# A diffusion transformer in two layers: the value-and-key projection in the score banks with early weights, adaLN tiles in pumps of three and in buffers of their own

## The chip, the cores and the metric

One NeuronCore of a Trainium2 chip runs the whole program as one launch. The metric is the device time of an execution in microseconds (us). Engines are TensorE (PE; its weight loads are PEld), VectorE (DVE), ScalarE (ACT), GpSimd (POOL) and SyncE (SP), which here only issues DMAs, in the order of its queue. Every engine executes its own instructions in order.

## The reference

Two layers of a diffusion transformer over 256 latent and 256 context tokens of width 1024. In each layer:

```
sa, ca, ga, sf, cf, gf = split(silu(c) @ w_ada + b_ada, 6)      # adaLN, also for c_ctx
h = layernorm(x) * (1 + ca) + sa                                # latent and context tokens
aq,ak,av, nq,nk,nv, cq, ckv, kr = split(h @ w_in)               # 2720 columns
group A (6 heads): two softmax maps, p1 - lam * p2, times av, rmsnorm
group B (6 heads): neighbourhood attention with bias, plus context keys
group C (4 heads): q = rmsnorm(cq) @ w_uq, k, v = rmsnorm(ckv) @ w_ukv, shared rotary key kr
x = layernorm(alpha * x + ga * (concat(A, B, C) @ w_out)) * g1 + b1
u = conv3(modulate(x, sf, cf) @ w_up); y = (silu(gate) * val) @ w_down
x = layernorm(alpha * x + gf * y) * g2 + b2
```

The context tokens take the same path in layer 0 (they read only context). The output is the latent stream.

## The kernel before

**Arithmetic.** Every large product is done in three matmuls (`mm3`): both operands are split into a rounded part (hi) and the remainder (lo), and hi*hi, lo*hi and hi*lo are summed. A weight block is loaded into a `raw` tile (128 x 1024 float32, 512 KB), ScalarE casts it to `whi`, VectorE subtracts to `wlo` (`wsplit`). There are 4 `raw` buffers and 3 each of `whi` and `wlo`. PSUM has 3 banks `acc`, one `ada`, 2 `sc` (scores) and 2 `tp` (transposes).

**adaLN.** w_ada comes in tiles of 128 x 1024. For layer 0 the tiles of round "b" (16) and "c" (8) are multiplied on TensorE (`ada`): a "b" tile is two matmuls on two of the four column groups of the array, and the tile of the other column half (`h`) uses the other two. For layer 1, rounds "b" (16), "c" (8) and "d" (8) run on VectorE in layer 0's w_down stage (`ada_vec`): one scalar_tensor_tensor a tile into an accumulator (the first of eight on ScalarE), and after eight tiles TensorE gathers the accumulator with small matmuls into a `tp` bank. `pump(n)` emits the work of the next n tiles; the projections pump `PF` tiles each, the w_down stage `DP` = 2 tiles a block in its first phase and 1 in its second. All these tiles share the four `raw` buffers with the weights.

**Order.** `ORDERS` lists by hand the parts of the attention of each layer (v: values, ck and cq: the compressed key and query of group C with their norms, mk and mq: its keys and queries, aq to bk: queries and keys of A and B, A, B, C: attention, f: the rest of the adaLN tiles). A list scheduler then sets the order on each engine, hoisting instructions past each other. Some sums ("early", `EF` and value block 0) are done while the tokens are still being modulated. `proj_vk` is the projection onto the last value columns and the rotary key of C: per token tile 24 matmuls with 288 columns, weights in three blocks (864, 864 and 576 columns).

**The w_down stage of layer 0** (`token_major`). The first phase sums the first 512 output columns for four token tiles at once, 11 blocks of w_down with 24 matmuls each. Then `gated` multiplies the sums by the gate and adds them into `xr` (two VectorE instructions a token tile), which frees the banks. The second phase takes the other 512 columns, in a pass over token tiles 2 and 3 (11 blocks of 12 matmuls) and one over 0 and 1, each closed by norm and modulation for layer 1.

## Time and profile before

| | us |
|---|---|
| median of 3 runs | 1173.5 |
| their range | 1173.08 to 1174.99 |
| the profiled execution, its own time | 1174.29 |
| its span in the trace | 1172.5 |
| TensorE busy in the span | 1112.0 |
| VectorE, ScalarE busy | 833.3, 590.3 |
| mean granted clock of TensorE | 0.985 |

Busy times are shares of the span that the engines spend on instructions; they overlap. TensorE is the fullest engine, so what counts is where it stands idle or slow, and what it waits for there. In the trace, names such as `raw<-in_w_ada` are destination and source of an instruction, L129 is a line of the kernel (129 to 131 are the three matmuls of `mm3`, 116 and 117 cast and subtraction of a split, 207 the VectorE step and 228 the TensorE matmul of an adaLN tile, 737 the norm's matmul with ones). TensorE's float32 matmuls are counted as several in the trace (x4 there is x2 in the program).

### The profile page before, as it was taken

How to read it: one execution, taken by the hardware profiler on the slowest of the kernel's cores; microseconds unless marked ns; L12 is line 12 of the kernel's file. 1: busy time of each engine (PE TensorE's matmuls, PEld its weight loads, DVE VectorE, ACT ScalarE, POOL GpSimd, SP SyncE). 2: the span in 40 equal slices, each digit the busy share in tenths (PEclk: the TensorE clock that was granted, in tenths of full speed). 3: DMA queues.
4: the chain of work that ended last, by engine and by line, in shares of the span. 5: the costliest groups of instructions: out<-in, count | busy, mean ns of one | idle time of the engine just before them, and what ended most of it. 6: DMA issues, size and time to landing. Idle time of an engine off the chain costs nothing.

```text
span 1172.5 us, 17767 instructions
## 1 busy us (share of the span) xinstructions
PE 1112.0 (95%) x6704; PEld 899.5 (77%) x6704; DVE 833.3 (71%) x1505; ACT 590.3 (50%) x1063; POOL 83.7 (7%) x104
## 2 busy tenths in 40 slices
PE   5999999999998999999999998989999978999997
PEld 4757766677778988887887776878778758999985
DVE  4533677767588986987975568774776777888755
ACT  4235566655548634444441224564664656666531
POOL 0001000003113000000000002120000411000000
PEclk9999999999999999999999999999999997999999
DMA  9487311112143653644548787523112343556562
GB/s 362 187 284 259 126 37 73 37 37 68 64 165 95 211 166 126 202 150 134 186 156 280 258 267 236 167 74 129 59 37 73 104 153 107 181 181 183 203 210 88
DMA packets 58196, 179.17 MB, mean 153 GB/s; under 512 B 7016, under 2 KB 12408, under 8 KB 58112
## 3 DMA queue, kind: packets, MB, share of 16 engines
q1 hardware_dynamic: 58112, 178.05, 45.8%
q8 instruction: 53, 0.87, 0.3%
q14 instruction: 31, 0.25, 0.1%
HBM read 176.94 MB, written 1.08 MB: 152 GB/s over the span
## 4 chain that ended last, share of the span: by engine, by line
PE 79%; DVE 7%; DMA 6%; ACT 3%; issue 3%; POOL 2%; SPq 1%; DVEq 0%; ACTq 0%; POOLq 0%
PE acc L129 20%; PE acc L130 20%; PE acc L131 20%; PE sc L605 6%; PE tp L385 3%; DMA raw<-in_w_down 3%; PE tp L393 3%; PE sc L810 2%; DVE adasc L207 1%; DVE wlo L117 1%; DMA raw<-in_w_ada 1%; ACT whi L116 1%; PE ada L228 1%; POOL xn L337 1%; DMA rawx<-in_w_ada_e 1%
## 5 line engine op out<-in xcount | busy, mean ns | idle before, releaser
L117 DVE TENSOR_TENSOR wlo<-raw,whi 128x1024 fp32r<-128x1024 f32 (+1 forms) x206 | 249.2, 1214 | 147.0 <-ACT whi L116 141.8
L116 ACT CAST whi<-raw 128x1024 fp32r<-128x1024 f32 (+1 forms) x206 | 212.9, 1038 | 264.6 <-PE acc L130 120.7
L129 PE MATMUL acc<-hhi,whi 128*128 128x256 f32 (+1 forms) x960 | 326.4, 341 | 3.6 <-ACT hhi L353 3.5
L130 PE MATMUL acc<-hlo,whi 128*128 128x256 f32 (+1 forms) x960 | 324.8, 339 | 0.5 <-DVE hlo L354 0.3
L131 PE MATMUL acc<-hhi,wlo 128*128 128x256 f32 (+1 forms) x960 | 323.5, 337 | 0.0
L129 PEld LDWEIGHTS acc<-hhi,whi 128*128 128x128 f32 x960 | 183.6, 192 | 28.6 <-issue 6.1
L130 PEld LDWEIGHTS acc<-hlo,whi 128*128 128x128 f32 x960 | 183.7, 192 | 22.3 <-issue 3.6
L131 PEld LDWEIGHTS acc<-hhi,wlo 128*128 128x128 f32 x960 | 183.6, 191 | 21.7 <-issue 4.1
L377 ACT ACTIVATE p<-sc,nm 128x512 f32<-128x512 f32 (+1 forms) x132 | 81.3, 618 | 25.6 <-DVE nm L374 24.1
L374 DVE TENSOR_REDUCE nm<-sc 128x1 f32<-128x512 f32 (+1 forms) x132 | 77.3, 597 | 19.8 <-PE sc L605 16.2
L386 ACT COPY pT<-tp 128x512 f32<-128x512 f32 (+1 forms) x96 | 49.4, 515 | 55.9 <-PE tp L385 55.3
L605 PE MATMUL sc<-stk,stq 32*128 32x512 f32 (+3 forms) x324 | 75.0, 392 | 1.1 <-ACT p L377 0.9
L605 PEld LDWEIGHTS sc<-stk,stq 32*128 32x128 f32 (+1 forms) x324 | 41.5, 183 | 26.4 <-issue 11.9
L1036 ACT ACTIVATE u<-acc,conv 128x256 f32<-128x256 f32 (+1 forms) x94 | 60.8, 647 | 1.4 <-PE acc L131 1.3
L1039 DVE SCALAR_TENSOR_TENSOR u<-acc,conv,u 128x255 f32<-128x255 f32 (+1 forms) x94 | 54.9, 584 | 4.6 <-ACT u L1036 4.6
L207 DVE SCALAR_TENSOR_TENSOR ac<-raw,scT,ac 128x1024 f32<-128x1024 f32 x42 | 53.3, 1278 | 5.8 <-DMA raw<-in_w_ada 5.8
L1040 DVE SCALAR_TENSOR_TENSOR u<-acc,conv,u 128x255 f32<-128x255 f32 (+1 forms) x94 | 55.3, 588 | 2.3
L385 PE MATMUL tp<-ident,p 128*128 128x128 f32 x320 | 52.7, 279 | 0.1
L130 PE MATMUL acc<-wlo,gBhi 128*128 128x512 f32 x133 | 52.2, 393 | 0.5 <-DVE mv L313 0.5
L385 PEld LDWEIGHTS tp<-ident,p 128*128 128x128 f32 x320 | 36.7, 140 | 20.5 <-issue 8.6
L131 PE MATMUL acc<-whi,gBlo 128*128 128x512 f32 x133 | 51.8, 391 | 0.0
L129 PE MATMUL acc<-whi,gBhi 128*128 128x512 f32 x133 | 51.8, 392 | 0.0
(265 smaller groups left out, 1814.6 us busy)
## 6 DMA issues: line engine op xcount, KB each, us to landing
raw<-in_w_up SPq DMA_DIRECT2D x94, 512.0 KB
raw<-in_w_ada SPq DMA_DIRECT2D x80, 512.0 KB
raw<-in_w_down SPq DMA_DIRECT2D x53, 512.0 KB
raw<-in_w_f SPq DMA_DIRECT2D x27, 512.0 KB
rawx<-in_w_ada_e SPq DMA_DIRECT2D x16, 512.0 KB
raw<-in_w_out SPq DMA_DIRECT2D x16, 512.0 KB
rpb<-in_rpb SPq DMA_DIRECT2D x24, 128.0 KB
gate<-scr SPq DMA_DIRECT2D x12, 256.0 KB
```

The source lines that it names most:

```text
L116: S.copy(hi, raw)
L117: V.tensor_tensor(lo, raw, hi.bitcast(F32), ALU.subtract)
L129: T.matmul(o, lhsT=lh, rhs=rh, start=first, stop=False)
L130: T.matmul(o, lhsT=lh, rhs=rl, start=False, stop=False)
L131: return T.matmul(o, lhsT=ll, rhs=rh, start=False, stop=last).ins
L207: V.scalar_tensor_tensor(ac[c], raw, s, ac[c], ALU.mult, ALU.add)
L374: V.reduce_max(nm, sc[:, 0:nk], axis=AX.X, negate=True)
L377: hT["exp"] = S.activation(p[:, 0:nk], sc[:, 0:nk], AF.Exp, bias=nm, accum_out=sums[:, 0:1]).ins
L385: T.transpose(pt[:, 128 * kc:128 * kc + 128], p[:, 128 * kc:128 * kc + 128], ident)
L605: T.matmul(sc[:, 0:nk], lhsT=q[r, a, qs], rhs=k[r, b, 0:nk], start=t == 0, stop=t == 2, tile_position=(r.start, 0))
L1036: S.activation(t, po[:, c], AF.Identity, scale=cw[:, 1:2], bias=cw[:, 3:4])
L1040: V.scalar_tensor_tensor(t3[:, :, 0:255], p3[:, :, 1:], cw[:, 2:3], t3[:, :, 0:255], ALU.mult, ALU.add)
```

## The change

- `PF` goes from 2 to 3. The early parts (`proj_v` and `fm` with sums from before) no longer pump.
- A new pool `ring` of eight tiles `rawr` takes the adaLN rounds e0, e1 and e3 of the start and then layer 0's "b" and "c" tiles, instead of the shared `raw`; `RX` drops to 4. Before the first attention part the remaining tiles are flushed, the ring is closed, and the attention output `mix` is allocated.
- `vk_weights` loads and rounds w_vk ahead: in layer 0 two of its blocks during the last early step, in layer 1 before the first part; the third block goes into `stk` tiles. `proj_vk` puts its sums into the score banks (in layer 1 alternately with `acc`).
- In the w_down stage the tiles of layer 1's adaLN get four buffers of their own, in the space of the second modulated half (`adalo`), with the accumulators in that of the first (`adahi`, before `adasc`).
- In `ORDERS`, layer 1 gets v1 ahead of mq and mk ahead of aq2; layer 0 loses its `f`.

```diff
--- before.py
+++ after.py
@@ -35,12 +35,13 @@
         ("cosk", "sink", "bones", "ones", "m01", "mneg"), ("st", "stq", "stk"), ("p0",), ("vt",))
 
 
-ORDERS = ("v0 ck cq v1 mk aq0 mq ak1 bq2 C1 ak0 aq1 C0 aq2 A0 bk1 ak2 A1 bk2 bq1 f A2 bk0 bq0 v2 B2 B0 W3 B1 W0 W1",
-          "cq v0 ck mq aq1 v1 aq2 mk ak0 ak1 C0 aq0 C1 ak2 f A1 bq0 bk1 A0 bk0 bk2 bq1 A2 bq2 v2 B0 B1 W3 W1 B2 W0")
+ORDERS = ("v0 ck cq v1 mk aq0 mq ak1 bq2 C1 ak0 aq1 C0 aq2 A0 bk1 ak2 A1 bk2 bq1 A2 bk0 bq0 v2 B2 B0 W3 B1 W0 W1",
+          "cq v0 ck v1 mq aq1 mk aq2 ak0 ak1 C0 aq0 C1 ak2 f A1 bq0 bk1 A0 bk0 bk2 bq1 A2 bq2 v2 B0 B1 W3 W1 B2 W0")
 EARLY = (0, 4)
-PF = 2
+PF = 3
 DP = (2, 1)
-RX = 12
+RX = 4
+RING = 8
 XB = (2, 2, 2, 3)
 HMB = (2, 2, 3, 2)
 PRE = ((0, 1),)
@@ -50,8 +51,12 @@
 
 
 class Slices:
-    def __init__(self, ap):
-        self.ap = ap
+    def __init__(self, ap, ring):
+        self.ap, self.ring = ap, ring
+
+    def raw(self, n):
+        self.ring.append(self.ring.pop(0))
+        return self.ring[-1]
 
     def tile(self, shape, dt, tag=None, name=None, bufs=1):
         o = {"ac0": 0, "ac1": 1024, "bada": 2048}[tag]
@@ -143,6 +148,9 @@
             r = mm3(po[:, 256 * e:256 * e + 256], hT["hi"][:, k, tok], hT["lo"][:, k, tok],
                     hi[:, k % 4, :], lo[:, k % 4, :], first and k == ks[0], last and k == ks[-1])
         return r
+
+    def vk_cols(l, k0, n):
+        return I["w_vk"][l, :, 288 * k0:288 * (k0 + n)]
 
     def kview(w, k):
         return [a.rearrange("p (k c) -> p k c", k=k) for a in w]
@@ -182,9 +190,9 @@
     adaT = {}
     garow = {}
 
-    def ada_w(l, r, k, h):
+    def ada_w(l, r, k, h, raw=wraw):
         c0 = ROUNDS[r][0]
-        raw = wraw(1024)
+        raw = raw(1024) if l or r == "d" else next_slot()
         src = I["w_ada"][l, k * P:(k + 1) * P]
         if r[0] == "a":
             src = src[:, 0:2048].rearrange("p (v s c) -> p s v c", v=2, s=2)[:, c0 // 512]
@@ -200,7 +208,7 @@
         for h in range(nh):
             ac = [ap.tile([P, 1024], F32, tag=f"ac{c}", name="ac", bufs=1) for c in conds]
             for k in range(KD):
-                raw = ada_w(l, r, k, h)
+                raw = ada_w(l, r, k, h, getattr(ap, "raw", wraw))
                 for c in conds:
                     s = scT[:, k, c:c + 1]
                     if k:
@@ -416,8 +424,11 @@
             shift(mv, rs)
             S.activation(xin[t], xin[t], AF.Identity, scale=rs[:, 0:1], bias=rs[:, 1:2])
 
+    def next_slot():
+        return ring.tile([P, 1024], F32, tag="rawr", name="rawr", bufs=RING)
+
     def load_round(s):
-        raws = [lp.tile([P, 1024], F32, tag="rawx", name="rawx", bufs=RX) for _ in range(4)]
+        raws = [lp.tile([P, 1024], F32, tag="rawx", name="rawx", bufs=RX) if s == 2 else next_slot() for _ in range(4)]
         for kp, raw in enumerate(raws):
             load(raw, I["w_ada_e"][s, kp])
         return raws
@@ -468,6 +479,8 @@
                 w[0][:, k % 2, 384:640], w[1][:, k % 2, 384:640], k == 0 and e == 0, k == KD - 1 and e == 1)
 
     new_h()
+    ring_st = ExitStack()
+    ring = pool(ring_st, "ring")
     load_x([2, 3])
     ebias = lp.tile([P, 512], F32, name="ebias")
     load(ebias, I["b_ada_e"])
@@ -493,6 +506,8 @@
         if s < 3:
             wes.append(load_early(s + 1))
             raws, nxt = nxt, load_round(s + 2) if s < 2 else None
+        if s == 3:
+            early["vk"] = {k0: kview(wsplit(vk_cols(0, k0, 3), 864), 3) for k0 in (0, 3)}
         if s == 0:
             for n in range(len(EF)):
                 for k in ks:
@@ -521,7 +536,7 @@
     for l in range(L):
         last = l == L - 1
         hst = ExitStack()
-        h2 = pool(hst, f"h2{l}")
+        mix = []
         lam_init = 0.8 - 0.6 * math.exp(-0.3 * l)
         qc = LAT if last else ALL
         nq = 256 if last else 512
@@ -548,7 +563,6 @@
         V.tensor_scalar_mul(nw[:, 0:1], K["nrm"][:, l, 0:1], 1.0 - lam_init)
         V.tensor_scalar_mul(nw[:, 1:3], K["nrm"][:, l, 1:3], C_SCALE)
 
-        mix = [h2.tile([P, KD, nq], F32R, tag=n, name="mix" + n) for n in ("hi", "lo")]
         core = ExitStack()
         ap = Pools([(pool(core, f"at{l}_{i}", "right"), keys) for i, keys in enumerate(CORE)])
         load_tables(ap)
@@ -563,21 +577,29 @@
             for kb in sorted({k // 4 for k in ks}):
                 w[kb] = w.get(kb) or kview(wsplit(I["w_v"][l, u, kb], 1024), 4)
             for pr in (1, 0):
-                pump(PF)
+                if not pos:
+                    pump(PF)
                 po = pos[pr] if pos else acc()
                 for e in range(2):
                     if pr in prs:
                         v_mm(po, w, ks, pr, e, ks[0] == 0, e == 1 or ks[0] == 0)
                 S.copy(vt[:, 2 * pr:2 * pr + 2, c0:c0 + 256], po.rearrange("p (t c) -> p t c", t=2))
 
+        def vk_weights():
+            vkw.update(early.pop("vk", None) or {k0: kview(wsplit(vk_cols(l, k0, 3), 864), 3) for k0 in (0, 3)})
+            raw = wraw(576)
+            load(raw, vk_cols(l, 6, 2))
+            hi, lo = (st_k().rearrange("p a c -> p (a c)")[:, 0:576] for _ in range(2))
+            split_from(raw, hi, lo)
+            vkw[6] = kview((hi, lo), 2)
+
+        vkw = {}
+
         def proj_vk():
-            w = {}
-            for k0 in (0, 3, 6):
-                n = min(3, KD - k0)
-                w[k0] = kview(wsplit(I["w_vk"][l, :, 288 * k0:288 * (k0 + n)], 288 * n), n)
+            w = vkw
             for t in (2, 3, 0, 1):
                 tok = slice(128 * t, 128 * t + 128)
-                po = acc()
+                po = acc() if last and t % 2 else scp()
                 for k in range(KD):
                     hi, lo = w[k // 3 * 3]
                     mm3(po[:, 0:288], hT["hi"][:, k, tok], hT["lo"][:, k, tok], hi[:, k % 3, :], lo[:, k % 3, :],
@@ -590,7 +612,6 @@
                 po, w, rest = early.pop(i)
                 k0 = 0 if w else 4
                 w = w or kview(wsplit(I["w_f"][l, i, :, 512:1024], 512), 4)
-                pump(PF)
                 for c, ks in rest:
                     f_mm(po, w, k0, ks, c, False, c == CTX)
                 return po
@@ -839,7 +860,14 @@
                  "ak": proj_ak, "bq": proj_bq, "bk": proj_bk, "A": attn_a, "B": attn_b, "C": attn_c, "f": flush}
         seq = ORDERS[l].split()
         for n, part in enumerate(seq):
+            if part[0] in "ABC" and not mix:
+                flush()
+                ring_st.close()
+                h2 = pool(hst, f"h2{l}")
+                mix.extend(h2.tile([P, KD, nq], F32R, tag=v, name="mix" + v) for v in ("hi", "lo"))
             cc["early"] = n < EARLY[l]
+            if not n:
+                vk_weights()
             parts[part.rstrip("0123")](*map(int, part[len(part.rstrip("0123")):]))
         with tc.issue_after(hT["exp"]):
             S.preload_act_table_set("silu_and_others")
@@ -1114,7 +1142,9 @@
         pq = pool(fst, f"pq{l}", "right")
         g2, b2 = lnrow(pq, "ln2_g", l), lnrow(pq, "ln2_b", l)
         if not last:
-            sc = Slices(h1.tile([P, KD, 512], F32R, tag="hi", name="adasc").bitcast(F32).rearrange("p k c -> p (k c)"))
+            free = [h1.tile([P, KD, 512], F32R, tag=n, name="ada" + n).bitcast(F32).rearrange("p k c -> p (k c)")
+                    for n in ("hi", "lo")]
+            sc = Slices(free[0], [free[1][:, 1024 * i:1024 * i + 1024] for i in range(4)])
             pend.extend([ada_vec(l + 1, "b", sc, (0,)), ada_vec(l + 1, "c", sc, (0,)), ada_vec(l + 1, "d", sc, (0,))])
 
         def head2(t):
```

Three places show how this moves instructions. The first is TensorE's order behind the early sums of layer 0 (`sc<-ehi`), before the change: adaLN tiles (`ada`), the norm's matmuls with `ones`, then the first of the w_vk sums (128x288).

```order
L131 MATMUL sc<-ehi,hlo 128x256
L228 MATMUL ada<-raw,scT 32x512 x8
L737 MATMUL tp<-csq,ones 128x512 x2
L228 MATMUL ada<-raw,scT 32x512 x4
L129 MATMUL acc<-whi,hhi 128x288
L737 MATMUL tp<-csq,ones 128x512
L130 MATMUL acc<-wlo,hhi 128x288
L131 MATMUL acc<-whi,hlo 128x288
```

And after it, the w_vk sums follow at once, into `sc`:

```order
L135 MATMUL sc<-elo,hhi 128x256
L136 MATMUL sc<-ehi,hlo 128x256
L134 MATMUL sc<-whi,hhi 128x288
L135 MATMUL sc<-wlo,hhi 128x288
L136 MATMUL sc<-whi,hlo 128x288
L134 MATMUL sc<-whi,hhi 128x288
L135 MATMUL sc<-wlo,hhi 128x288
```

The first adaLN matmuls now come behind 48 such sums (x4, that is two tiles), then x6, x6, and, among the sums of a later part, three tiles cut into pieces:

```order
L136 MATMUL acc<-whi,stk 128x256
L236 MATMUL ada<-rawr,scT 32x512
L134 MATMUL acc<-whi,stk 128x256
L135 MATMUL acc<-wlo,stk 128x256
L136 MATMUL acc<-whi,stk 128x256
L236 MATMUL ada<-rawr,scT 32x512 x4
L134 MATMUL acc<-whi,stk 128x256
L135 MATMUL acc<-wlo,stk 128x256
L136 MATMUL acc<-whi,stk 128x256
```

So tiles that came in pairs now come in threes, and those of one pump are split by the scheduler. In all 12 "b" tiles stand behind the early sums, before and after.

The second place is the w_down stage of layer 0. SyncE's queue before, behind the first three adaLN tiles of the stage, takes blocks and tiles in turn:

```order
L105 DMA raw<-in_w_ada 128x1024
L105 DMA raw<-in_w_down 128x1024
L105 DMA raw<-in_w_ada 128x1024 x2
L105 DMA ln_g<-in_ln_g 128x1024
L105 DMA ln_b<-in_ln_b 128x1024
L105 DMA raw<-in_w_down 128x1024
L105 DMA raw<-in_w_ada 128x1024 x2
L105 DMA raw<-in_w_down 128x1024
L105 DMA raw<-in_w_ada 128x1024 x2
```

After it, the loads from the last of w_up on are:

```order
L110 DMA raw<-in_w_up 128x1024
L110 DMA raw<-in_w_down 128x1024 x6
L110 DMA adalo<-in_w_ada 128x1024 x5
L110 DMA ln_g<-in_ln_g 128x1024
L110 DMA ln_b<-in_ln_b 128x1024
L110 DMA adalo<-in_w_ada 128x1024 x5
L110 DMA raw<-in_w_down 128x1024
L110 DMA adalo<-in_w_ada 128x1024 x2
L110 DMA raw<-in_w_down 128x1024
```

Six blocks go ahead of the first tile, and the first `adalo` waits for the last matmul that reads the second modulated half, at the end of w_up. In VectorE's order the end of the first phase was, with the split of a block (`wlo`), adaLN steps (`adasc`) and the gated sums (`gate`, `xr`):

```order
L117 TENSOR_TENSOR wlo<-raw,whi 128x1024
L207 SCALAR_TENSOR_TENSOR adasc<-raw,scT,adasc 128x1024
L117 TENSOR_TENSOR wlo<-raw,whi 128x1024
L869 TENSOR_TENSOR acc<-acc,gate 128x512
L207 SCALAR_TENSOR_TENSOR adasc<-raw,scT,adasc 128x1024
L870 SCALAR_TENSOR_TENSOR xr_3469,rsum<-xr_3469,acc 128x512
L869 TENSOR_TENSOR acc<-acc,gate 128x512
L869 TENSOR_TENSOR ada<-ada,gate 128x512
```

and is now:

```order
L215 SCALAR_TENSOR_TENSOR adahi<-adalo,scT,adahi 128x1024 x2
L122 TENSOR_TENSOR wlo<-raw,whi 128x1024
L215 SCALAR_TENSOR_TENSOR adahi<-adalo,scT,adahi 128x1024 x3
L122 TENSOR_TENSOR wlo<-raw,whi 128x1024
L215 SCALAR_TENSOR_TENSOR adahi<-adalo,scT,adahi 128x1024
L897 TENSOR_TENSOR acc<-acc,gate 128x512 x2
L898 SCALAR_TENSOR_TENSOR xr_3473,rsum<-xr_3473,acc 128x512
L898 SCALAR_TENSOR_TENSOR xr_3475,rsum<-xr_3475,acc 128x512
L897 TENSOR_TENSOR ada<-ada,gate 128x512
```

An adaLN step stood between the first gated sum and its addition into `xr`; now the last step stands ahead of all the gated sums, and three steps stand ahead of the split before it.

The third place is TensorE's order at the start of layer 1. Before, behind the last early value sums (`sc<-hhi`), came the norm's matmul and the queries of C (`acc<-stq`):

```order
L129 MATMUL sc<-hhi,whi 128x256
L130 MATMUL sc<-hlo,whi 128x256
L131 MATMUL sc<-hhi,wlo 128x256
L737 MATMUL tp<-csq,ones 128x512
L129 MATMUL acc<-stq,whi 128x256 x3
L130 MATMUL acc<-stq,whi 128x256
```

After it the w_vk sums follow, and the norm's matmul stands among them:

```order
L136 MATMUL sc<-whi,hlo 128x288
L134 MATMUL sc<-whi,hhi 128x288
L135 MATMUL sc<-wlo,hhi 128x288
L758 MATMUL tp<-csq,ones 128x512
L136 MATMUL sc<-whi,hlo 128x288
L134 MATMUL sc<-whi,hhi 128x288
L135 MATMUL sc<-wlo,hhi 128x288
```

The queries of C (`acc<-stq`) now come behind all 96 w_vk sums; the first of those stands directly behind the early sums.

## Rows read from the trace of the kernel before

**Rows 1.** The page: busy us of engines, share of span, instructions.

```profile
PE 1112.0 (95%) x6704; PEld 899.5 (77%) x6704; DVE 833.3 (71%) x1505; ACT 590.3 (50%) x1063; POOL 83.7 (7%) x104
```

**Rows 2.** Windows: busy us (instructions) by engine, granted clock, DMA share, GB/s.

```profile
50.00:75.00 25.00, 22.11 (x120) 12.57 (x118) 7.97 (x20) 8.31 (x16) 0.00 (x0) 0.99 0.61 198
400.00:425.00 25.00, 25.00 (x112) 20.72 (x111) 23.59 (x28) 9.86 (x14) 0.00 (x0) 1.00 0.64 198
775.00:800.00 25.00, 20.71 (x142) 19.46 (x141) 14.64 (x27) 12.35 (x26) 5.38 (x6) 0.93 0.31 93
```

**Rows 3.** TensorE timeline after the early sums: start, us, tiles, count, [idle <-releaser].

```profile
65.17 2.46 PE L228 MATMUL ada<-raw,scT 128*32 128x512 f32 x16
67.87 1.96 PE L737 MATMUL tp<-csq,ones 128*128 128x512 f32 x4 [0.24 <-DMA ones<-in_ones]
70.44 1.05 PE L228 MATMUL ada<-raw,scT 128*32 128x512 f32 x4 [0.61 <-DMA raw<-in_w_ada]
71.74 1.05 PE L228 MATMUL ada<-raw,scT 128*32 128x512 f32 x4 [0.25 <-DMA raw<-in_w_ada]
73.90 0.37 PE L129 MATMUL acc<-whi,hhi 128*128 128x288 f32 x1 [1.10 <-ACT whi L116]
74.95 2.07 PE L737 MATMUL tp<-csq,ones 128*128 128x512 f32 x2 [0.69 <-ACT csq L734]
77.06 0.44 PE L131 MATMUL acc<-whi,hlo 128*128 128x288 f32 x1
...
78.21 0.30 PE L130 MATMUL acc<-wlo,hhi 128*128 128x288 f32 x1
...
80.55 1.06 PE L228 MATMUL ada<-raw,scT 128*32 128x512 f32 x8
81.55 0.40 PE L129 MATMUL acc<-whi,hhi 128*128 128x288 f32 x1
```

**Rows 4.** Timeline of TensorE in layer 0's w_down stage, its begin, middle and end.

```profile
607.41 0.50 PE L129 MATMUL acc<-whi,gAhi 128*128 128x512 f32 x1
...
669.79 0.39 PE L129 MATMUL acc<-whi,gChi 128*128 128x512 f32 x1
...
671.60 0.39 PE L131 MATMUL acc<-whi,gClo 128*128 128x512 f32 x1
675.53 0.76 PE L129 MATMUL acc<-whi,gAhi 128*128 128x512 f32 x1 [3.54 <-DVE xr L870]
...
711.74 0.61 PE L131 MATMUL acc<-whi,gClo 128*128 128x512 f32 x2
```

**Rows 5.** Waits of TensorE from 600 to 750 us: total, times, longest.

```profile
PE tp L215 <- DVE adasc L207: 1.5, 2, 1.2
```

**Rows 6.** Timeline of VectorE at the end of the first phase.

```profile
672.12 0.69 DVE L869 TENSOR_TENSOR acc<-acc,gate 128x512 f32<-128x512 f32 x1
673.49 1.28 DVE L207 SCALAR_TENSOR_TENSOR adasc<-raw,scT,adasc 128x1024 f32<-128x1024 f32 x1 [0.67 <-DMA raw<-in_w_ada]
```

**Rows 7.** Windows of 5 us in the same stage, columns as before.

```profile
620.00:625.00 5.00, 5.00 (x23) 4.14 (x23) 0.47 (x2) 0.00 (x0) 0.00 (x0) 1.00 0.99 322
675.00:680.00 5.00, 4.47 (x13) 3.61 (x14) 5.00 (x11) 0.00 (x0) 0.00 (x0) 0.66 0.80 270
```

**Rows 8.** DMA view, 600 to 712 us: what was moved.

```profile
DMA packets 8339, 28.81 MB, mean 257 GB/s; under 512 B 931, under 2 KB 1187, under 8 KB 8335
...
raw<-in_w_ada SPq DMA_DIRECT2D x30, 512.0 KB
```

**Rows 9.** Timeline of SyncE's queue: when adaLN tiles are asked for.

```profile
586.95 5.68 SPq L105 DMA_DIRECT2D raw<-in_w_ada  x2
```

**Rows 10.** Waits of TensorE from 764 to 812 us.

```profile
PE acc L129 <- ACT stq L121: 2.7, 1, 2.7
PE tp L737 <- ACT csq L734: 1.5, 1, 1.5
PE sc L810 <- DVE stk L370: 0.8, 1, 0.8
```


## The prediction

> **What bounds the kernel now.** I began with the busy line of the page: TensorE is at work for 1112.0 of the 1172.5 us of the span [rows 1], so nothing else can be worth more than some 60 us, and a change that leaves TensorE's work alone can only fill holes. The second view was the busy time in windows, to see where the holes are. A window of the middle is full, 25.00 of 25 us, while 50 to 75 holds 22.11 and 775 to 800 only 20.71 [rows 2]; what is gained before a full window is carried through it to the end, because TensorE has no slack there to give back. The third view was TensorE's timeline in the three places that the diff touches: the start of layer 0, the w_down stage of layer 0, the start of layer 1.
>
> Start of layer 0: between 65.17 us, where the early sums end, and 77.06, where the key-and-value sums at last run on, there are five idle spells, of 0.24, 0.61, 0.25, 1.10 and 0.69 us, for the table of ones, for adaLN tiles, for the rounded w_vk and for the squares of the norm [rows 3].
>
> The w_down stage of layer 0: its first matmul is at 607.41, the first of the second half at 675.53 behind a wait of 3.54 us for the gated sum, the last of the pass over tokens 2 and 3 at 711.74 and 0.23 later, twice, so that the pass ends near 712.2 [rows 4]. At full clock eight matmuls lie between 669.79 and 671.60, 0.226 us each. The work is 11 x 24 = 264 matmuls, 59.7 us, and 11 x 12 = 132, 29.9 us: dense, it would end at 697.0. So 15.2 us are lost. What is known of them: 3.7 from 671.8 to 675.5; a wait for the adaLN accumulator, 1.2 at the longest [rows 5]; and a granted clock of 0.66 from 675 to 680 [rows 7], which is the lower level, 1.2 GHz, for two thirds of the window, right after the idle spell.
>
> Start of layer 1: waits of 2.7, 1.5 and 0.8 us [rows 10].
>
> **The start of layer 0.** The change puts the 96 sums of w_vk straight behind the early sums and moves the six adaLN tiles and the norm's ones-matmuls among and behind them. What the 11.9 us from 65.17 to 77.06 hold as work: six tiles, which at the price of a pair (80.55 to 81.55, 1.00 us for two tiles [rows 3]) are 3.0; six ones-matmul passes at 1.96 / 4 = 0.49, 2.9; two first key sums, 0.3. That is 6.2, so 5.7 are there to be won if everything is ready in time. It should be: w_vk no longer stands behind adaLN tiles in SyncE's queue, and the three casts and three subtractions that move ahead fit into 50 to 75, where VectorE works 7.97 and ScalarE 8.31 of 25 us [rows 2]. If they came in the way of the modulated tokens there, up to 2 us would go.
>
> Against it stands the pump of three. Two "b" tiles share one pass, as they use different column groups: two tiles take 1.06 us (80.55), and a lone tile takes 1.05 (70.44, 71.74) [rows 3]. By the order 12 such tiles follow after the early sums; in pumps of two they are 6 passes, in pumps of three (pair and lone, lone and pair) and with the one that the scheduler splits 9. Three passes more at 1.00 are 3.0 us. The copies out of the score banks have a cover: two banks alternate, and a bank has 3.1 us before it is wanted again (the other's 24 sums; 17 of them go from 78.21 to 80.55, 0.13 to 0.14 each [rows 3]); without that it is some 0.5 us at two places, which I leave at nothing. Net gain: 5.7 - 3.0 = **2.7 us**, between 0 and 5.7.
>
> **The w_down stage.** What is removed is the shared buffer: adaLN tiles no longer hold back w_down blocks, nor blocks tiles. What is added is a late start: the tiles lie where the second modulated half was, so that the first can be asked for only after the last w_up matmul, near 607.4; before, the first two were asked for at 586.95 [rows 9]. And VectorE's order changes: the gated sum stands, as before, behind an adaLN step that waits for its tile, now that of tile 23. Behind that step are queued the four gated sums, then the subtractions for blocks 14 and 15; TensorE waits for the first sum into xr, as only that frees its bank.
>
> So when is tile 23 there? Ahead of it in SyncE's queue after 607.4 are 22 tiles, two ln rows and w_down blocks 7 to 15: with itself 34 transfers of 0.524 MB (512 KB, [rows 8]) and a bias of 0.26, together 18.1 MB. They begin to flow near 609 (1.5 us allowed for the queue; each us more or less moves the result by as much). The rate is the open price. Over 600 to 712 the mean is 257 GB/s [rows 8], but that has gaps, as queue and buffers wait for each other; a window with the engines busy 0.99 of the time moved 322 [rows 7]. I take 300, nearer the full window since four buffers keep the queue filled, and keep 270 and 322 for the range. At 300 the tile lands at 609 + 60.3 = 669.3; the step takes 1.28, the gated sum 0.69 [rows 6], and the next one and the sum into xr behind it about as much, 0.6 from start to start: TensorE goes on near 672.6 instead of 675.5. Then 29.9 us of pass, 1.5 for the same drop of the clock (two thirds of 5 us at half speed), and about 2 for blocks whose subtraction stands behind an adaLN step: 706.0 instead of 712.2. Gain: **6.2 us**. At 322 the tile lands at 665.2, ahead of the end of the first half at 667.1; some 0.5 between the halves, no drop: 699.5, gain 12.7. At 270 it lands at 676.0, TensorE goes on at 679.4, and with 4 us of waits the pass ends at 714.8: 2.6 lost. The tail of the stage (norm, modulation, both as before) I leave as it is.
>
> The Trainium skill, "DMA: Bandwidth & Descriptors", section Bandwidth, gives 341 GB/s for one megabyte and 425 for sixteen, and some 358 as the limit of a core at the memory. The trace's full window, 322, is close below the first. By 341 the tile would land at 662 (an estimate), and the whole would come to 1154.1, as at 322.
>
> **The start of layer 1.** The value-and-key sums, 96 of 0.13 us, now stand between the early sums and the first sums that need the normed query; the ones-matmul comes after 11 of them. So the waits of 2.7 and 1.5 us get 12.5 us of cover, and the 0.8 of the first score goes, since w_vk no longer follows the keys: 5.0. Something is late next: a score row of the C heads now stands right behind the key sums and waits for their rotation and copies; I take 1.0 for it, from the 0.8 that such a wait costs now [rows 10]. If w_vk's cast is late (it needs the buffer of an early weight block) up to 1 more. Gain **4.0 us**, between 3.0 and 5.0.
>
> **Sum.** 2.7 + 6.2 + 4.0 = 12.9 us. The profiled run took 1174.3, 0.8 over the median of three (1173.5). 1174.3 - 12.9 = 1161.4, and on the median's scale 1160.6.
>
> **The rivals.**
> - *The transfers run full.* At 322 GB/s or more the w_down stage gives 12.7: 1160.6 - 6.5 = 1154.1. For it: the windows of 322. Against it: blocks stand in one queue with tiles, and each waits for its buffer in turn. (The skill's figures above would make it this one.)
> - *The transfers stay near 270.* The late start and the wait for tile 23 then eat the stage's gain: 2.6 lost instead of 6.2 gained, 1169.4; halfway, 285 GB/s, it is near 1165. For it: the mean of 257. Against it: that mean has idle gaps.
> - *The first stage gives nothing*, its 5.7 going to lone tiles, a late table and late casts: 1163.3.
> - *No change to speak of*: the holes are filled by others of the same size, 1171.2 to 1175.8 (0.2% either way is about what a measurement here can tell from none).
> - *Slower, by one mechanism*: the adaLN tiles of the w_down stage become its bound. The place is VectorE's queue at the gated sum and then each subtraction behind a tile. It decides where the rate makes the pass end later than 712.2 + 6.7 + 2.3 = 721.2, what the other two stages give and the 0.2% together: the tiles may then take 721.2 - 609 - 3.3 - 29.9 - 1.5 - 5 of waits = 72.5 us for 18.1 MB, or 250 GB/s, just under the mean of now. At 240 tile 23 lands 3 us later still, and the time is 1179. For it: 32 tiles now begin 20 us later. Against it: in [rows 7] the engines move 322 when asked.
>
> **Chances.** My forecast (1157 to 1163) 0.42; full transfers 0.16; transfers near 270 or halfway 0.17; first stage nothing 0.11; no change 0.06; slower 0.08. Faster: 0.86. Most cases have one sign, so one range does: from 1153.5, where the full rate lies, up to 1169, which leaves out no change, slower and a little at either end, some 2 in 10.
>
> **What would show it.** In the changed kernel: no adaLN pass or ones-matmul between the last early sum and the first w_vk sum, the latter in score banks and without a wait for its cast; lone "b" tiles of 1.05 us; the first w_down-stage tile asked for after the last w_up matmul; the wait ahead of the second half down to some 2 to 5 us, its releaser an xr sum that followed a late tile; 5-us windows of 300 GB/s and more from 610 to 660; no wait for stq or csq at the start of layer 1. The prediction is wrong if those windows stay near 257, if the early casts delay the modulated tokens, or if the C score row waits 3 us instead of 1.

## The result, and the profile after

| | before | changed |
|---|---|---|
| median, on one chip (us) | 1174.24 | 1157.24 |
| range, number of runs | 1173.08 to 1178.36, 4 | 1156.11 to 1158.32, 4 |
| the profiled execution, its own time | 1174.29 | 1158.32 |
| its span in the trace | 1172.5 | 1156.2 |

The ratio of the times is 0.9858, interval 0.9841 to 0.9875: 17.0 us faster by the medians, 16.0 between the profiled executions, where the sum had 12.9.

The busy line of the page, to be read against [rows 1]:

```profile
PE 1108.7 (96%) x6704; PEld 899.0 (78%) x6704; DVE 833.7 (72%) x1505; ACT 590.0 (51%) x1063; POOL 85.2 (7%) x104
```

The same number of instructions on each engine, 3.3 us less of TensorE's time, and a span shorter by 16.3. So 13.0 us of the gain are holes that were filled. The other 3.3 go with a higher clock: its mean went from 0.985 to 0.988, which means 17.6 us lost to the lower clock before and 13.9 now (an estimate from these means and the spans).

To see which holes, I cut both traces at the same instructions on TensorE. Stretch A runs from the last early sum to the first w_down matmul, B from the first to the last w_down matmul of layer 0, C from the last early sum of layer 1 to the first matmul with w_out behind it. Each is the difference of two start times in the timeline (us):

| kernel | A | B | C |
|---|---|---|---|
| before | 542.45 | 139.45 | 141.06 |
| changed | 537.08 | 129.68 | 138.49 |
| gain | 5.4 | 9.8 | 2.6 |
| gain forecast | 2.7 | 6.2 | 4.0 |

The three gains make 17.7 before rounding; 1.0 goes because the last early sum starts at 65.97 instead of 64.96, 0.4 behind C. (Nothing shows that this 1.0 is a price of the early casts: the traces of all the experiments lie between 64.73 and 66.40 there, and the two that cast late, 1 and 6, have 65.68 and 65.63.)

**Start of layer 0.** TensorE's timeline, answering to [rows 3]: start, us, tiles, count.

```profile
65.97 0.28 PE L136 MATMUL sc<-ehi,hlo 128*128 128x256 f32 x1
66.22 0.40 PE L134 MATMUL sc<-whi,hhi 128*128 128x288 f32 x1
...
70.83 1.88 PE L758 MATMUL tp<-csq,ones 128*128 128x512 f32 x4
...
74.50 1.06 PE L236 MATMUL ada<-rawr,scT 128*32 128x512 f32 x8
...
79.83 1.91 PE L236 MATMUL ada<-rawr,scT 128*32 128x512 f32 x12
...
85.04 1.91 PE L236 MATMUL ada<-rawr,scT 128*32 128x512 f32 x12
...
89.19 1.04 PE L236 MATMUL ada<-rawr,scT 128*32 128x512 f32 x2
...
90.72 1.07 PE L236 MATMUL ada<-rawr,scT 128*32 128x512 f32 x8
...
92.61 1.04 PE L236 MATMUL ada<-rawr,scT 128*32 128x512 f32 x2
```

No idle spell is marked; from 60 to 130 us TensorE waits for nothing. A pump of two tiles (x8) takes 1.06 us, one of three (x12) 1.91, and even the half of a tile that the scheduler split off (x2, one of its two matmuls) takes 1.04.

**The w_down stage.** TensorE, answering to [rows 4], then VectorE, to [rows 6].

```profile
603.05 0.50 PE L134 MATMUL acc<-whi,gAhi 128*128 128x512 f32 x1
...
665.93 0.39 PE L136 MATMUL acc<-whi,gClo 128*128 128x512 f32 x1
666.43 0.47 PE L134 MATMUL acc<-whi,gAhi 128*128 128x512 f32 x1
...
697.28 0.39 PE L136 MATMUL acc<-whi,gClo 128*128 128x512 f32 x1
697.60 0.64 PE L223 MATMUL tp<-adahi,scT 128*32 128x256 f32 x8
```

```profile
663.18 1.28 DVE L215 SCALAR_TENSOR_TENSOR adahi<-adalo,scT,adahi 128x1024 f32<-128x1024 f32 x1
664.38 1.31 DVE L897 TENSOR_TENSOR acc<-acc,gate 128x512 f32<-128x512 f32 x2
665.60 0.68 DVE L898 SCALAR_TENSOR_TENSOR xr<-xr,acc 128x512 f32<-128x512 f32 x1
```

The second half starts without a wait. The step of tile 23, at 663.18, stands ahead of the gated sums as the order had it, but starts as soon as VectorE is free, with no idle time marked in front of it: the tile was there. The first sum into xr is done at 666.28, in the moment in which the first half's last matmul ends (665.93 + 0.39). The DMA view from 603 to 697, and windows (columns as in [rows 2]):

```profile
DMA packets 8538, 29.56 MB, mean 315 GB/s; under 512 B 948, under 2 KB 1204, under 8 KB 8533
```

```profile
50.00:75.00 25.00, 25.00 (x158) 19.15 (x157) 8.96 (x26) 7.46 (x16) 0.00 (x0) 1.00 0.50 174
628.00:653.00 25.00, 25.00 (x112) 19.77 (x111) 14.13 (x14) 5.36 (x5) 0.00 (x0) 1.00 0.81 295
653.00:678.00 25.00, 24.88 (x115) 19.79 (x113) 20.71 (x25) 6.69 (x7) 0.00 (x0) 1.00 0.91 315
775.00:800.00 25.00, 23.09 (x126) 19.87 (x125) 16.20 (x36) 14.82 (x31) 2.62 (x3) 0.86 0.40 127
```

The windows that held 22.11 in layer 0 and an idle spell in the w_down stage are full, or all but 0.12 us, at granted clock 1.00. The fourth is not: it holds 23.09 instead of 20.71, but at clock 0.86 instead of 0.93. (The changed kernel is 14 us ahead by then, so these two windows hold different parts of the start of layer 1; stretch C compares like with like.) What TensorE waits for at the start of layer 1 (735 to 812 us), answering to [rows 10]:

```profile
PE sc L831 <- ACT stk L793: 1.8, 1, 1.8
PE sc L135 <- DVE mv L321: 1.4, 1, 1.4
PE tp L348 <- POOL xn L345: 1.3, 1, 1.3
```

The last two are as before; those for stq, csq and the rotated key (2.7, 1.5 and 0.8) are gone, and one of 1.8 us for the keys of group C has come.

### The profile page after: what moved, and what is told of

Read it like the earlier page. It is cut to its first block, busy times and chain, and to the rows that moved or that the text cites. A ratio compares the mean times of both kernels' runs of the same rounds, so it can differ in the third digit from the quotient of the medians.

```text
span 1156.2 us, 17757 instructions
## 1 busy us (share of the span) xinstructions
PE 1108.7 (96%) x6704; PEld 899.0 (78%) x6704; DVE 833.7 (72%) x1505; ACT 590.0 (51%) x1063; POOL 85.2 (7%) x104
## 4 chain that ended last, share of the span: by engine, by line
PE 88%; DVE 5%; POOL 2%; ACT 2%; issue 2%; DMA 1%; SPq 0%; DVEq 0%; POOLq 0%; ACTq 0%
PE acc L134 22%; PE acc L135 21%; PE acc L136 21%; PE sc L626 6%; PE tp L393 3%; PE tp L401 3%; PE sc L831 2%; PE ada L236 1%; PE sc L134 1%; PE sc L135 1%; PE sc L136 1%; DVE wlo L122 1%; POOL xn L345 1%; POOL rs L323 1%; DMA rawr<-in_w_ada_e 1%
## 5 line engine op out<-in xcount | busy, mean ns | idle before, releaser
L121 ACT CAST whi<-raw 128x1024 fp32r<-128x1024 f32 (+3 forms) x204 | 211.6, 1042 | 252.4 <-PE acc L135 127.0
L122 DVE TENSOR_TENSOR wlo<-raw,whi 128x1024 fp32r<-128x1024 f32 (+3 forms) x204 | 247.2, 1216 | 120.2 <-ACT whi L121 117.4
```

Of the source, the lines that this page charges most:

```text
L121: S.copy(hi, raw)
L122: V.tensor_tensor(lo, raw, hi.bitcast(F32), ALU.subtract)
```

## The experiments

Times are medians with their range; the ratio is to the kernel before on the same chip in the same rounds. The kernel before had 1172.86, 1172.2 and 1173.38 beside experiments 1 to 4, 5 to 8 and 9 to 12.

**1. Own buffers alone.** The kernel before, with nothing of the change but the buffers of the w_down stage.

```diff
...
+            free = [h1.tile([P, KD, 512], F32R, tag=n, name="ada" + n).bitcast(F32).rearrange("p k c -> p (k c)")
+                    for n in ("hi", "lo")]
+            sc = Slices(free[0], [free[1][:, 1024 * i:1024 * i + 1024] for i in range(4)])
```

> The kernel before with one part of the change: layer 1's adaLN tiles of the w_down stage in four buffers of their own. Theory 1 (the shared buffers held both queues back, and full transfers keep up with the late start): the distance between the traces grew by 9.8 us in this stage, so about 1174.2 - 9.8 = 1164.4 us, the first matmul of the second half without a wait, windows of 350 GB/s and more right after the last w_up matmul. Theory 2 (the stage gained because what stands ahead of it changed, earlier loads above all): the part alone gives less than half, 1169 us or more, and the wait of 3.5 us at the start of the second half comes back.

Measured: 1166.64 (1164.64 to 1167.59, 6 runs), ratio 0.9938 (0.9916 to 0.9959). B is 129.66 us, as in the changed kernel, A and C nearly as before (541.42, 141.14). All that TensorE waits for from 600 to 740:

```profile
PE tp L344 <- POOL xn L341: 1.3, 1, 1.3
PE acc L134 <- DVE mv L317: 0.6, 1, 0.6
```

So the whole of stretch B comes from the buffers and needs nothing of the rest: theory 1, though the time is 2.2 us over its 1164.4. The medians give 6.2 us, the trace 9.8 in B. Part of that gap is which executions were profiled: the one of the kernel before took 1174.29, 1.4 over its median here, and this one 1164.64, 2.0 under its own. How long B is in the other executions is not shown.

**2. The changed kernel without the own buffers.**

```diff
-                raw = ada_w(l, r, k, h, getattr(ap, "raw", wraw))
+                raw = ada_w(l, r, k, h, wraw)
```

> The changed kernel with this one part undone: the tiles of the w_down stage again in the shared buffers. Theory 1: 1157.2 + 9.8 = 1167 us, the wait of about 3.5 us between the halves is back. Theory 2 (the rest of the change carries it): it stays below 1162 us.

Measured: 1165.25 (1159.08 to 1167.67, 6 runs), ratio 0.9929 (0.9904 to 0.9954), 8.0 us over the changed kernel's median above and 9.4 over that of experiment 5: theory 1. The profiled run was the fastest of the six; in it B is 135.06 us, with these waits from 600 to 740:

```profile
PE acc L134 <- DVE xr L898: 1.9, 1, 1.9
...
PE acc L134 <- ACT whi L121: 1.3, 1, 1.3
```

The waits for the gated sum (1.9 us in this fast run, where 3.5 was expected) and for a rounded block come with the shared buffers and go with the own ones.

**3. Pumps of four.** Two whole pairs in each pump instead of a pair and a lone tile.

```diff
-PF = 3
+PF = 4
```

> The changed kernel with pumps of four tiles instead of three, so that b tiles come in pairs again. Theory 1 (a lone tile costs a pass of 1.0 us as a pair does): 6 passes instead of 9 behind the early sums, 3 us less, about 1154.2 us. Rival (the passes were hidden in waits that TensorE would have had anyway, or tiles of four come too late from memory): within 0.5 us of the changed kernel, with waits for adaLN tiles in the trace.

Measured: 1152.24 (1151.96 to 1152.98, 4 runs), ratio 0.9817 (0.9792 to 0.9842). A is 533.70, 3.4 us less than with three; B and C are as they were (129.69, 136.82). The first two pumps in TensorE's timeline:

```profile
74.16 1.92 PE L236 MATMUL ada<-rawr,scT 128*32 128x512 f32 x16
...
80.41 1.92 PE L236 MATMUL ada<-rawr,scT 128*32 128x512 f32 x16
```

Four tiles take 1.92 us, three took 1.91: the lone tile's pass is paid in full and buys half as much. That is theory 1: the time is 3.6 us under that of experiment 5. This version beats both kernels.

**4. Layer 1 as before.** Order, time of the weights and banks of layer 1 put back.

```diff
-          "cq v0 ck v1 mq aq1 mk aq2 ak0 ...
+          "cq v0 ck mq aq1 v1 aq2 mk ak0 ...
...
+            if last:
+                vk_weights()
...
-                po = acc() if last and t % 2 else scp()
+                po = acc() if last else scp()
...
-            if not n:
+            if not n and not last:
                 vk_weights()
```

> The changed kernel with the start of layer 1 as before: parts in the old order, w_vk loaded and rounded where it is used, sums in the accumulator banks. Theory 1 (the part won 2 us, since the 5 us of waits were covered but a wait of 1.8 us and a lower clock at the first scores came instead): 1159.2 us, waits of 2.7 and 1.5 us for stq and csq back, and the wait of 1.8 us at the first scores gone. Rival (the part won its full 5 us and something else was lost in layer 1): 1162 us.

Measured: 1161.09 (1159.39 to 1163.1, 6 runs), ratio 0.9893 (0.9871 to 0.9914). C is 141.25, as before, and the old waits are back (740 to 815):

```profile
PE acc L134 <- ACT stq L126: 2.6, 1, 2.6
PE tp L760 <- ACT csq L757: 1.5, 1, 1.5
...
PE sc L833 <- DVE stk L378: 0.9, 1, 0.9
```

The wait of 1.8 us is gone; at the first scores stand 0.9, where the kernel before had 0.8. Layer 1's part is thus worth 3.9 us against the first median of the changed kernel and 5.2 against that of experiment 5, on this chip. That is the rival; theory 1, which gave it 2, fell.

**5. The changed kernel again**, to have it beside the others on their chip.

> The changed kernel itself, as the measure for the other runs on the same chip: 1156 to 1159 us; w_down stage of 129.7 us from its first to its last matmul in the trace, whatever the transfers do.

Measured: 1155.86 (1154.85 to 1156.21, 4 runs), ratio 0.9856 (0.9838 to 0.9873), just under the 1156 expected. A 537.24, B 129.72, C 136.81: the first two repeat to 0.2 us, C is 1.7 shorter than in the first trace. The same 1.8 us wait is there, but what follows runs at another clock:

```profile
775.00:800.00 25.00, 23.25 (x133) 19.82 (x133) 17.92 (x39) 15.71 (x32) 2.63 (x3) 0.93 0.38 127
```

**6. Layer 0 as before, with the ring.** w_vk late and in `acc` banks, pumps of two, pumps in the early parts again; the ring of eight tiles stays.

```diff
...
-        if s == 3:
-            early["vk"] = {k0: kview(wsplit(vk_cols(0, k0, 3), 864), 3) for k0 in (0, 3)}
...
-                po = acc() if last and t % 2 else scp()
+                po = acc() if not last or t % 2 else scp()
```

> The changed kernel with the start of layer 0 as before except for the ring of eight tiles: w_vk loaded and rounded where it is used, its sums in the accumulator banks, pumps of two, pumps also among the early parts. Theory 1 (what the start of layer 0 won, 4.4 to 5.4 us in the traces, comes from w_vk being there early): about 1162 us, the waits for whi and csq before the first w_vk sums back. Rival (it comes from the ring, whose tiles are loaded earlier): within 1.5 us of the changed kernel, 1158.5 us at most, no waits for adaLN tiles.

Measured: 1162.46 (1159.82 to 1164.37, 6 runs), ratio 0.9912 (0.9894 to 0.993). A is 544.05, 6.8 us longer than in experiment 5. Of these, 5.0 stand ahead of the first matmul with w_out in layer 0 (205.28 us behind the last early sum, against 200.26), and 1.8 behind it, where the granted clock from 350 to 360 us was 0.83. Waits from 60 to 130:

```profile
PE ada L236 <- DMA rawr<-in_w_ada: 1.6, 1, 1.6
PE acc L134 <- DVE cy L771: 1.0, 2, 0.7
PE tp L252 <- DVE adarow L247: 0.8, 1, 0.8
```

The ring alone does not take the waits for adaLN tiles away; with w_vk's sums in front of them they are gone. The time is that of theory 1, but its sign failed: no wait for whi or csq came back. As four things were put back together, this run does not say what each is worth.

**7. Two own buffers instead of four.** The transfers then wait for VectorE more often; the question was whether the rate has anything to spare.

```diff
-            sc = Slices(free[0], [free[1][:, 1024 * i:1024 * i + 1024] for i in range(4)])
+            sc = Slices(free[0], [free[1][:, 1024 * i:1024 * i + 1024] for i in range(2)])
```

> The changed kernel with two own buffers instead of four in the w_down stage. Theory 1 (what counts is that tiles and blocks no longer share buffers; the transfers have rate to spare): no more than 1 us over the changed kernel, the w_down stage still 129.7 to 131 us. Rival (the rate is what the stage lives on and needs four transfers in flight, as the prediction took it): the stage 4 us longer or more, a wait between its halves, 1161 us or more.

Measured: 1168.61 (1166.96 to 1169.19, 6 runs), ratio 0.9962 (0.9948 to 0.9977). B is 142.51, 3 us longer than before the change. TensorE's waits from 600 to 720, the DMA view from 603 to 712, and two windows to be held against those of the changed kernel above:

```profile
PE tp L223 <- DVE adahi L215: 5.3, 2, 3.1
PE acc L134 <- DVE xr L898: 2.2, 2, 1.8
```

```profile
DMA packets 8521, 29.51 MB, mean 271 GB/s; under 512 B 944, under 2 KB 1200, under 8 KB 8517
```

```profile
628.00:653.00 25.00, 20.98 (x91) 16.05 (x89) 12.51 (x12) 5.36 (x5) 0.00 (x0) 1.00 0.75 260
653.00:678.00 25.00, 23.36 (x91) 17.59 (x92) 15.30 (x21) 4.30 (x4) 0.00 (x0) 0.86 0.68 226
```

The rate falls to 260 and 226 GB/s, VectorE waits 11 times for a tile from 600 to 700 us, and TensorE behind it loses time idle and then in clock. My theory, that the rate had something to spare, fell; the rival held. One more thing differs: with two buffers the next w_down block stands behind two tiles in SyncE's queue, with four behind ten, and what that order costs by itself was not measured. This is the prediction's rival of transfers near 270 GB/s: it had a stage 2.6 us longer and a time of 1169.4 for it, and here are 271 GB/s, 3.1 and 1168.6. That the times agree so closely is in part chance, since A and C give 5.0 and 5.5 us in this trace, where the forecast had 2.7 and 4.0.

**8. Pumps of four, keys of group C ahead of its queries**, against the new wait in layer 1.

```diff
-          "cq v0 ck v1 mq aq1 mk aq2 ak0 ...
+          "cq v0 ck v1 mk aq1 mq aq2 ak0 ...
```

> The changed kernel with pumps of four, and in layer 1 the keys of C ahead of its queries (mk ahead of aq1 and mq), which puts some 100 matmuls between them and their first scores. Theory 1 (the wait of 1.8 us at the first score and the lower clock after it are what the start of layer 1 gave back): 2 to 3 us less than with pumps of four alone (1152.2), about 1149.5 us, no wait for stk, and the window 775 to 800 at full clock. Rival (the keys themselves now wait for their norm): a wait of 1 us or more for stk at the key sums, 1151 to 1153 us.

Measured: 1152.98 (1152.59 to 1154.98, 4 runs), ratio 0.9836 (0.9818 to 0.9854), no better than pumps of four alone. The wait of 1.8 us is gone, and these came in its place (740 to 815):

```profile
PE acc L134 <- ACT stq L130: 1.3, 1, 1.3
...
PE acc L134 <- ACT stk L802: 1.2, 2, 1.0
```

The window 775 to 800 shows clock 1.00 here, and still C is 136.93: the wait moved, its price stayed. Theory 1 fell, the rival held.

**9. Three own buffers** (`range(3)` in the line of experiment 7).

> The changed kernel with three own buffers in the w_down stage. If the gain of the stage depends on how many transfers are in flight, three lie between two (1168.6) and four (1155.9): 1158 to 1164 us, the stage 131 to 138 us long, VectorE's waits for adaLN tiles between 2.5 us (four) and 16.9 us (two). If two were slow for the order that the scheduler made of them alone, three are as fast as four, 1157 us at most.

Measured: 1156.36 (1155.94 to 1156.86, 4 runs), ratio 0.9857 (0.9838 to 0.9877). B is 130.55. VectorE does wait for tiles, but TensorE only 0.7 us for a gated sum:

```profile
DVE adahi L215 <- DMA adalo<-in_w_ada: 12.3, 8, 2.7
```

The same line had 16.9 us with two buffers and has 2.5 with four (all three from 600 to 700). Three hide nearly all of it: the step lies between two and three. The first of the two expectations was right on VectorE's waits and wrong on the time, for which it had 1158 to 1164; the time is that of the second. So fewer buffers do cost VectorE time, but with three it has that time to spare.

**10. Pumps of four and six own buffers**, two more in unused columns of the first half.

```diff
-            sc = Slices(free[0], [free[1][:, 1024 * i:1024 * i + 1024] for i in range(4)])
+            sc = Slices(free[0], [free[1][:, 1024 * i:1024 * i + 1024] for i in range(4)]
+                        + [free[0][:, o:o + 1024] for o in (1024, 2560)])
```

> Pumps of four and six own buffers (two more in the part of the accumulators' half that lies idle). If four buffers already make the stage TensorE's (129.7 us, of which 89.6 are w_down sums of the first three quarters), six change nothing: 1151.5 to 1153 us. If a few waits are left for tiles, 1 to 2 us less, with VectorE's waits for tiles gone.

Measured: 1152.18 (1150.77 to 1153.3, 4 runs), ratio 0.9821 (0.98 to 0.9842); B 129.71. More buffers bring nothing.

**11. Layer 1's order alone**, with its w_vk loaded and rounded only when its part comes (the lines on `vk_weights` in experiment 4's diff).

> The changed kernel with layer 1's w_vk loaded and rounded where it is used, the new order of parts kept. If the order of the parts makes the cover (the loads are hoisted by the scheduler anyway), within 1 us of the changed kernel (1155.9). If the early rounding is needed, a wait of 1 us or more for its cast ahead of the first w_vk sums, 1157 to 1160 us.

Measured: 1156.51 (1155.58 to 1156.96, 4 runs), ratio 0.9858 (0.9838 to 0.9877), the same as the changed kernel; C 137.33. In layer 1 it is the order that covers the waits (the banks of the sums stayed as changed); early weights add nothing that these runs can tell.

**12. Pumps of four again**, on the chip of experiments 9 to 11.

> Pumps of four once more, beside the others of this call: 3 us less than the changed kernel's 1155.9, 1152 to 1153.5 us.

Measured: 1153.18 (1151.95 to 1155.57, 5 runs), ratio 0.9831 (0.981 to 0.9853); A 533.62. It is 3.3 us better than experiment 11 on this chip, as experiment 3 was 3.6 better than 5 on the other.

## Why the prediction was right, step by step

The time came out 3.4 us under the forecast, well inside the range and at the edge of the forecast's own 1157 to 1163. What the change takes away was right in all three stages. Three sizes were off, and in the w_down stage the wait that the forecast still left did not come. That the time stayed between 1157 and 1163 is partly luck: the first two stages gave 6.3 us more than forecast, and 1.4 too little in layer 1 and 1.4 outside the three stretches went against that.

*What bounds the kernel.* That TensorE is the bound and a hole filled early is carried to the end held: the three gains, 17.7, arrive at the end of the span as 16.3, less only the 1.0 and 0.4 named above.

*Start of layer 0: 2.7 forecast, 5.4 found.* The minus of three lone passes was right: experiment 3 takes them out and A falls by 3.4, against 3.0. So the plus was 8.7 instead of 5.7. I had counted what lay between 65 and 77 us and stopped there. Left out were a low clock just behind, 77.06 to 78.02 in the trace before, worth some 0.4, and waits of 0.2 and 0.4 at 97.7 and 98.7, which are gone as well. That makes 6.7. Of the other 2, half was not won in this stage at all. Up to the first matmul with w_out in layer 0 (269.59 us before, 266.27 changed) the gain is 4.3; the last 1.0 comes behind it. There the trace before has a spell at the lower clock, 1.2 GHz (granted clock 0.50 from 359 to 361 us), and the trace after has none. The windows from 355 to 365 us before, in the changed kernel and in experiment 1:

```profile
355.00:365.00 10.00, 8.80 (x58) 8.59 (x59) 8.56 (x19) 6.74 (x14) 1.88 (x2) 0.83 0.01 2
355.00:365.00 10.00, 10.00 (x85) 10.00 (x85) 8.35 (x22) 7.50 (x14) 5.32 (x5) 1.00 0.30 88
355.00:365.00 10.00, 7.92 (x64) 7.62 (x64) 9.68 (x22) 8.23 (x16) 2.07 (x2) 1.00 0.08 27
```

Experiment 1, which leaves the start of layer 0 alone, lacks the spell too, and its A is 1.0 shorter than before; so this 1.0 does not need the change of this stage. What sets the spell off was not found (experiment 6 has one there). Another 1 us stays open. No delay of the modulated tokens by the early casts shows, and no wait of TensorE for the copies out of the score banks, as taken.

*The w_down stage: 6.2 forecast, 9.8 found.* Two terms were mis-sized. The first is the rate, 300 GB/s: 315 from 603 to 697. By the prediction's own formula, 18.1 MB then take 57.5 us instead of 60.3, and tile 23 is there 59.1 us after the stage's first matmul; its step starts at 60.1. That alone would not remove the wait: the step and the sums behind it end 63.2 us after that matmul, and the prediction's first half was over at 59.7. But the first half takes 63.3, and this is the second term. My dense floor of 89.6 counted the w_down matmuls alone and forgot those that gather the adaLN accumulators, among them:

```profile
625.27 1.05 PE L223 MATMUL tp<-adahi,scT 128*32 128x512 f32 x4
```

They are no waits and stay, so some of the 15.2 us that the prediction called lost was work. With both, the sum into xr is ready when the first half ends, and there is neither the wait nor the drop of the clock, priced at 1.5 us. TensorE goes on 63.4 us after its first matmul, where the forecast had 65.2, and the rest of the pass takes 31.1 instead of 33.4. In this stage it was thus the rival of full transfers that came true, at a lower rate than I gave it; the wait of 2 to 5 us that was named as a sign did not show. That the stage did not give the 12.7 of that rival comes mainly from the gathers: the pass over tokens 2 and 3, begun at 603.05 and ended 0.23 after 697.28, takes 94.5 us at full clock, where I had 92.1 for that case. How the stage hangs on the rate was right at the other end as well: experiment 7 has the 270 of the lower bound, and its loss.

What transfers of this size reach at most stood in the trace before, but not where I looked: in the start-up they move 409 GB/s:

```profile
20.00:30.00 10.00, 10.00 (x116) 8.95 (x116) 4.87 (x9) 4.27 (x5) 0.14 (x1) 1.00 1.02 409
```

My 300 leaned on a window of 322 as if that were the most the queue can do. It came near the 315 for another reason: the queue of the changed kernel moves up to 414 GB/s too, and stands still in between (see the last section). The 341 GB/s that the Trainium skill gives for transfers of one megabyte ("DMA: Bandwidth & Descriptors", section Bandwidth) lies between 322 and 409: the stage's mean of 315 does not reach it, the start-up goes beyond.

*Start of layer 1: 4.0 forecast, 2.6 in the first trace, 4.2 in that of experiment 5.* The cover of 5.0 came as said. The new wait stands where it was put, at the C score row, with 1.8 instead of 1.0; by the medians of experiments 4 and 5 the part is worth 5.2. The first trace was short of that because of the clock behind the wait.

*The sum by parts.* By the medians of one chip: own buffers 6.2 put in alone (experiment 1) and 9.4 taken out alone (2 against 5), layer 1's part 5.2 (4 against 5), layer 0's 6.6 (6 against 5). Together they make 18.0 to 21.2, where the whole gives 16.3. So the parts add up only roughly; medians that move by 1 to 2 us, as the two of the changed kernel do (1157.24 and 1155.86), cannot say how much they hang on each other.

## What to carry to other kernels

Where a matmul uses only part of the array, count passes and not tiles: emit them in such numbers that every pass is full, since a pass for one tile costs what a pass for two does (three tiles 1.91 us, four 1.92). Where a stream of weights feeds a slower chain, give it buffers of its own and find the smallest depth at which the engine behind it stops waiting; here two lost, three won and six added nothing. And before a rate is taken from a row, look through the whole trace for the fullest window of the same kind of transfer, and then for what will stall the queue: here the fullest windows moved 409 to 414 GB/s, and the stage 315.

## What the runs showed that was not expected

**Transfers.** Windows of 5 us in the changed kernel, with 512 KB transfers:

```profile
605.00:610.00 5.00, 5.00 (x24) 4.13 (x23) 4.99 (x9) 2.71 (x3) 0.00 (x0) 1.00 1.02 390
640.00:645.00 5.00, 5.00 (x24) 4.14 (x23) 2.49 (x3) 1.05 (x1) 0.00 (x0) 1.00 1.03 414
```

These 390 and 414 GB/s are well over the 322 of the fullest window that I had read before. The stage's 315 is thus a mean of windows like these and of others in which SyncE's queue stands still. One such window of the changed kernel, and the queue's longest single wait from 603 to 697 us (total, times, longest):

```profile
647.00:652.00 5.00, 5.00 (x24) 3.23 (x23) 1.92 (x3) 1.35 (x2) 0.00 (x0) 1.00 0.33 102
```

```profile
SPq L110 <- DVE adahi L247: 8.7, 2, 7.7
```

For 7.7 us the queue stands at the store of a gate row (`scr<-adahi`, at 650.06), which waits for VectorE's sum of a gathered accumulator, and all loads queue up behind it. The Trainium skill, "HBM Reference", section Specifications (TRN2), gives the 358 that the prediction cited another meaning than I did: it says that 358 is a core's share when both cores of a pair stream, and that a core alone has measured about 425. This program runs on one core, and its 414 lies over the share and under the 425.

**The clock.** After the same wait of 1.8 us at the start of layer 1, the granted clock from 775 to 800 us was 0.86 in the first trace of the changed kernel, 0.93 in that of experiment 5, and 1.00 in that of experiment 2, which has the same code there. C is 138.49, 136.81 and 135.50: the lower the clock, the longer. In experiment 4, with the older and longer waits, the low spell comes earlier, in the first of its two windows. Experiment 2, then experiment 4:

```profile
775.00:800.00 25.00, 23.08 (x154) 20.66 (x153) 17.32 (x36) 16.32 (x32) 2.63 (x3) 1.00 0.35 115
```

```profile
750.00:775.00 25.00, 20.92 (x143) 19.55 (x143) 18.24 (x32) 15.70 (x31) 5.39 (x6) 0.86 0.22 63
775.00:800.00 25.00, 23.90 (x157) 21.81 (x156) 12.27 (x24) 11.87 (x25) 2.68 (x3) 1.00 0.40 133
```

What decides between them was not found.

**Spread.** Kernels with shared buffers in the w_down stage vary by 5.1 to 8.6 us between runs (the kernel before by 5.1 to 8.4 in its four sets of 4 to 11 runs, experiment 2 by 8.6 in 6), those with own buffers by 0.9 to 4.6 in 4 to 6 runs.
